# The norms' reciprocal root: Newton's rounds on GpSimd, both columns in one instruction

## The chip, the cores and the metric

The kernel runs on one core of a Trainium2 chip. Its engines are TensorE (PE in the profile; its weight loads are PEld), VectorE (DVE), ScalarE (ACT), GpSimd (POOL) and SyncE (SP, which only issues transfers here). They share SBUF; matmul results land in PSUM, which GpSimd doesn't use here. Each engine takes its instructions in the order in which they were queued, and waits on semaphores for the others. The metric is the device time of one execution in microseconds (us), the median of several runs.

## The reference, cut to what matters

Two transformer blocks run one after the other on 256 tokens of width 1024, the first with a second stream of 256 context tokens. Each has two layers. All of them normalise their input with

```python
def rms_norm(x, g):
    xf = x.astype(jnp.float32)
    y = xf * lax.rsqrt(jnp.mean(xf * xf, axis=-1, keepdims=True) + NORM_EPS)
    return (y * g.astype(jnp.float32)).astype(x.dtype)
```

For each token, then, one mean of squares and one reciprocal square root. The rest (attention of several kinds, gates, feed-forward layers) is matmuls with weights of 1024 rows and more, in float32.

## The kernel before

The residual streams lie in SBUF with the channels on the partitions: x is eight tiles of 128 channels x 256 tokens, xc is the same for the context. A weight is loaded as a raw tile and split into two parts of reduced precision, whi (a cast on ScalarE, line 200) and wlo (raw minus whi on VectorE, line 201); activations are split in the same way into hi and lo. product (lines 204 to 209) adds three matmuls for each block of 128 channels: whi with hi, whi with lo, wlo with hi. TensorE spends nearly all its time on these.

A norm goes like this. add_square sums the squares of the stream's tiles into one or two tiles sq. token_sums (line 263) brings them over the partitions with matmuls against a column of ones, so that sm holds two columns of 128 tokens each. stats_rstd (lines 266 to 274) turns them into var, -0.5 times mean plus epsilon, and calls rsqrt_columns: a start value from the bits of var by a shift and a subtraction on integers (tiles rc_s and rc_y, lines 249 and 250), and three rounds of Newton. A round is two instructions for each column, one that makes a = y * h * y (line 253) and one that makes y = (a + 1.5) * y (line 255); h is var. Then spread (line 279) transposes each column, broadcast to 128 x 128, on TensorE, so that sm holds the root of every token on all partitions, and norm (lines 311 to 317) multiplies: nt on VectorE reads sm, ScalarE makes hi, VectorE lo.

stats_rstd runs eight times, called P1 to P8 in what follows. P1 (383 us) and P2 (398 us) are the second norm of the first block's first layer, for x and for xc. P3 (764 us) and P4 (778 us) are the first norm of its second layer. P5 (993 us) is its second norm, in inner_raw, where the feed-forward matmuls start on the raw x and the root is multiplied in afterwards (fg, line 965). P6 (1216 us) and P8 (1520 us) are norms of a 128-channel key tile in the second block's two layers (ckv, line 1116). P7 (1494 us) is the norm of the second block's second layer, which is multiplied in later too. Three more calls of rsqrt_columns, one at the program's start, one between the blocks and one for the output, don't go through stats_rstd.

The order of each engine's queue isn't written out by hand. A framework schedules the program with its own estimates of how long instructions take, and code in tc.high_priority (the body of stats_rstd, wsplit) is drawn ahead of other work. So the queues can be ordered otherwise when an instruction changes its engine. The framework also sets the waits: an instruction on GpSimd that reads what the GpSimd instruction before it wrote waits for that one's semaphore.

The functions that the diff touches, and their callers:

Of the kernel before, what the change touches and what calls it, by code (L numbers as in the profile page):

```python
# [14 lines left out]
ALU = mybir.AluOpType  # L15
# [55 lines left out]
def two_blocks(ctx: ExitStack, tc: tile.TileContext, A, out: bass.AP, tap=None):  # L71
    nc = tc.nc
    V, SC, PE, GP = nc.vector, nc.scalar, nc.tensor, nc.gpsimd
# [166 lines left out]
            V.scalar_tensor_tensor(out=y, in0=a, scalar=1.5, in1=y, op0=ALU.add, op1=ALU.mult)  # L240
        return y

    def rsqrt_columns(h, name):

        n = h.shape[-1]
        sh = small.tile([P, n], I32, name=f"rc_s_{name}", tag=f"rc_s_{name}")
        y, a = (small.tile([P, n], F32, name=f"rc_{t}_{name}", tag=f"rc_{t}_{name}") for t in "ya")

        V.tensor_scalar(out=sh, in0=h.bitcast(I32), scalar1=1, scalar2=None, op0=ALU.logical_shift_right)
        V.tensor_scalar(out=y.bitcast(I32), in0=sh, scalar1=-1.0, scalar2=1597463007.0 + 1069547520.0, op0=ALU.mult, op1=ALU.add)  # L250
        for _ in range(3):
            for i in range(n):
                V.scalar_tensor_tensor(out=a[:, i:i + 1], in0=y[:, i:i + 1], scalar=h[:, i:i + 1], in1=y[:, i:i + 1], op0=ALU.mult, op1=ALU.mult)
            for i in range(n):
                V.scalar_tensor_tensor(out=y[:, i:i + 1], in0=a[:, i:i + 1], scalar=1.5, in1=y[:, i:i + 1], op0=ALU.add, op1=ALU.mult)
        return y

    def token_sums(tiles, b, c0=0, nt=2):

        for m, sq in enumerate(tiles):  # L260
            for i in range(nt):

                PE.matmul(b[:, c0 + i:c0 + i + 1], lhsT=sq[:, i * P:(i + 1) * P], rhs=ones[:, 0:1],
                          start=m == 0 and i == 0 and c0 == 0, stop=m == len(tiles) - 1, skip_group_check=True)

    def stats_rstd(tiles, denom, name="n"):

        b = sm_bank()
        token_sums(tiles, b)

        with tc.high_priority(offset=400):
            v = small.tile([P, 2], F32, name="var", tag="var")
            V.tensor_scalar(out=v, in0=b[:, :2], scalar1=-0.5 / denom, scalar2=-0.5 * EPS, op0=ALU.mult, op1=ALU.add)
            return rsqrt_columns(v, name)

    def spread(o, r, nt):

# [23 lines left out]
    def norm(s, hs, gain, shift=None, rstd=None, R=None):  # L301

        if R is None:
            r = stats_rstd(sumsq[s, 0], D) if rstd is None else rstd
            R = sm_bank()
            spread(R, r, 2)
        sl = slice(s * S, (s + 1) * S)
        for k in range(KD):
            t = narrow_tile("nt")
            hi, lo = hs[0][k][:, sl], hs[1][k][:, sl]  # L310
            V.scalar_tensor_tensor(out=t, in0=streams[s][k], scalar=gain(k), in1=R[:, :S], op0=ALU.mult, op1=ALU.mult)
            if shift is None:
                SC.copy(out=hi, in_=t)
                V.tensor_sub(out=lo, in0=t, in1=hi.bitcast(F32))
            else:
                SC.activation(out=hi, in_=t, func=AF.Identity, bias=shift(k), scale=1.0)  # L316
                V.scalar_tensor_tensor(out=lo, in0=t, scalar=shift(k), in1=hi.bitcast(F32), op0=ALU.add, op1=ALU.subtract)
# [130 lines left out]
    v = small.tile([P, 4], F32, name="var2", tag="var2")  # L448
# [5 lines left out]
    V.tensor_add(out=v, in0=v, in1=mv[:, :, 1])  # L454
    V.tensor_scalar(out=v, in0=v, scalar1=-0.5, scalar2=-0.5 * EPS, op0=ALU.mult, op1=ALU.add)
    r4 = rsqrt_columns(v, "f")
    Rp = pt_bank()
    spread(Rp, r4, 4)
# [208 lines left out]
    for l in range(DEPTH):  # L667
# [262 lines left out]
        for part, (f0, fn) in enumerate(((0, 8), (8, 8), (16, 6))):  # L930
            us = ([], [])
            for j2 in range(fn // 2):
# [18 lines left out]
                def inner_raw(u):  # L951

                    hi, lo = tiles[u]
                    bg, bu = acc()[:, :S + 2], sc_bank()[:, :S + 2]
                    product(bg, ws[2 * u], raws, KD, slice(0, S + 2))
                    product(bu, ws[2 * u + 1], raws, KD, slice(0, S + 2))
                    if not Rs:
                        R = sm_bank()
                        spread(R, stats_rstd(sumsq[0, 0], D), 2)
                        Rs.append(wide("Rs")[:, :S])  # L960
                        SC.copy(out=Rs[0], in_=R[:, :S])
                    cc = small.tile([P, 2], F32, name="shifts", tag="shifts")
                    g, t = wide("fg")[:, :S], wide("ft")[:, :S]
                    V.tensor_copy(out=cc[:, 0:1], in_=bg[:, S:S + 1])
                    V.tensor_mul(out=g, in0=bg[:, :S], in1=Rs[0])
                    SC.activation(out=g, in_=g, func=AF.Identity, bias=cc[:, 0:1], scale=1.0)
                    SC.activation(out=t, in_=g, func=AF.Tanh, scale=0.5)
                    V.scalar_tensor_tensor(out=t, in0=t, scalar=1.0, in1=g, op0=ALU.add, op1=ALU.mult)
                    V.tensor_copy(out=cc[:, 1:2], in_=bu[:, S:S + 1])
                    V.tensor_mul(out=g, in0=bu[:, :S], in1=Rs[0])  # L970
                    V.scalar_tensor_tensor(out=t, in0=g, scalar=cc[:, 1:2], in1=t, op0=ALU.add, op1=ALU.mult)
                    SC.copy(out=hi[:, :S], in_=t)
                    V.tensor_sub(out=lo[:, :S], in0=t, in1=hi[:, :S].bitcast(F32))
# [36 lines left out]
    v = small.tile([P, 4], F32, name="var2", tag="var2")  # L1010
    V.tensor_scalar(out=v, in0=b[:, :4], scalar1=-0.5 / D, scalar2=None, op0=ALU.mult)
    V.tensor_scalar(out=v[:, 0:2], in0=v[:, 0:2], scalar1=-0.5 * EPS, scalar2=None, op0=ALU.add)
    V.scalar_tensor_tensor(out=v[:, 2:4], in0=v[:, 0:2], scalar=EPS, in1=v[:, 2:4], op0=ALU.mult, op1=ALU.add)
    r4 = rsqrt_columns(v, "f")
    b1s.close()


    with tc.tile_pool(name="b2", bufs=1) as b2:
# [47 lines left out]
        for l in range(DEPTH):  # L1066
# [6 lines left out]
            if l == 0:  # L1073
                norm(0, hs, lambda k: gfw[:, k:k + 1], rstd=r4[:, 2:4])
                R = y_bank()
                spread(R, r4, 2)
            else:
                r4 = stats_rstd(sumsq[0, 0], D)
                norm(0, hs, lambda k: g_norm_2[1][:, k:k + 1], rstd=r4)
# [471 lines left out]
```

## Time and profile before

| What | Value |
|---|---|
| median of 3 runs | 1812.01 us (1809.88 to 1813.35) |
| profiled execution | 1806.31 us, its span 1804.5 us |
| TensorE busy | 1757.9 us (97%) |
| VectorE busy | 1304.5 us (72%), 2791 instructions |
| ScalarE busy | 913.8 us (51%) |
| GpSimd busy | 36.8 us (2%), 67 instructions |
| mean granted TensorE clock | 0.993 of full speed |

The profiled execution is one run; its span lasts from the first instruction to the last. Busy shares are of the span. TensorE's matmuls overlap, and their ends are modelled, so the start-to-start distance says more than the duration of one. The GpSimd rows are its constants, its transfers, sixteen small copies and eight subtractions.

### The profile page before, as it was taken

To read this page: it belongs to the slowest core of one execution; us is meant where nothing else is said; L and a number is where in the kernel's file an instruction comes from. 1 tells how busy PE (TensorE), PEld (TensorE's weight loads), DVE (VectorE), ACT (ScalarE), POOL (GpSimd) and SP (SyncE) were. 2 spreads that over 40 slices of the span, in tenths; PEclk is the share of its full clock that TensorE was granted. 3 is DMA by queue.
4 is the path that set the end of the run, shared out by engine and by line. 5 is a ranking of instruction groups with operands and counts; after the bars stand their busy time and mean duration, and the time that the engine had idled before them with its cause. 6 is when DMAs were issued, how large, how long until landed. Compare 5 with 4: busy or idle time off the path is not lost.

```text
span 1804.5 us, 29803 instructions
## 1 busy us (share of the span) xinstructions
PE 1757.9 (97%) x11553; PEld 1512.7 (84%) x11553; DVE 1304.5 (72%) x2791; ACT 913.8 (51%) x1728; POOL 36.8 (2%) x67
## 2 busy tenths in 40 slices
PE   7999999999999999999899999999999999999998
PEld 3666677798888888877699999988999998999996
DVE  6887877984657555698657756689876777986775
ACT  2578873333212212357755544465665456475444
POOL 1000000000000000000000000002000000100000
PEclk9999999999999999999999999999999999999999
DMA  9342426532444444434237455556535555544453
GB/s 315 114 111 65 129 86 167 175 129 94 140 146 163 153 155 155 145 107 142 87 105 204 157 190 187 164 163 186 164 122 164 164 187 164 177 142 135 151 187 117
DMA packets 248061, 270.89 MB, mean 150 GB/s; under 512 B 17886, under 2 KB 208720, under 8 KB 247920
## 3 DMA queue, kind: packets, MB, share of 16 engines
q1 hardware_dynamic: 246736, 267.28, 47.1%
q0 software_dynamic: 1184, 1.71, 0.6%
q8 instruction: 91, 1.49, 0.3%
q14 instruction: 50, 0.41, 0.1%
HBM read 267.90 MB, written 1.06 MB: 149 GB/s over the span
## 4 chain that ended last, share of the span: by engine, by line
PE 78%; DVE 10%; DMA 6%; ACT 4%; issue 2%; SPq 0%; ACTq 0%; DVEq 0%
PE acc L207 16%; PE acc L208 16%; PE acc L209 16%; PE sc L209 4%; PE sc L207 4%; PE sc L208 4%; DMA raw<-in_w_ffn_up_dram 3%; DVE wlo L201 3%; PE sc L590 3%; PE y L652 2%; PE pt L646 2%; ACT whi L200 2%; PE acc L1041 1%; PE acc L1040 1%; PE acc L1039 1%
## 5 line engine op out<-in xcount | busy, mean ns | idle before, releaser
L200 ACT CAST whi<-raw 128x1024 fp32r<-128x1024 f32 (+2 forms) x416 | 396.6, 959 | 601.0 <-PE acc L208 313.8
L201 DVE TENSOR_TENSOR wlo<-raw,whi 128x1024 fp32r<-128x1024 f32 (+2 forms) x416 | 458.7, 1109 | 212.3 <-ACT whi L200 207.0
L207 PE MATMUL acc<-hi,whi 128*128 128x256 f32 (+1 forms) x1920 | 590.4, 308 | 4.4 <-ACT hi L316 3.2
L208 PE MATMUL acc<-lo,whi 128*128 128x256 f32 (+1 forms) x1920 | 587.9, 307 | 0.1
L209 PE MATMUL acc<-hi,wlo 128*128 128x256 f32 (+1 forms) x1920 | 586.9, 306 | 0.9 <-DVE wlo L201 0.9
L207 PEld LDWEIGHTS acc<-hi,whi 128*128 128x128 f32 x1920 | 362.0, 189 | 25.5 <-issue 4.6
L208 PEld LDWEIGHTS acc<-lo,whi 128*128 128x128 f32 x1920 | 362.0, 189 | 19.9 <-issue 3.0
L209 PEld LDWEIGHTS acc<-hi,wlo 128*128 128x128 f32 x1920 | 362.2, 189 | 19.0 <-issue 2.4
L209 PE MATMUL sc<-hi,wlo 128*128 128x256 f32 (+1 forms) x392 | 130.5, 333 | 0.2 <-DVE wlo L201 0.2
L207 PE MATMUL sc<-hi,whi 128*128 128x256 f32 (+1 forms) x392 | 130.7, 333 | 0.0
L208 PE MATMUL sc<-lo,whi 128*128 128x256 f32 (+1 forms) x392 | 130.5, 333 | 0.0
L418 DVE SCALAR_TENSOR_TENSOR araw<-araw,silu 128x512 f32<-128x512 f32 x140 | 104.4, 746 | 26.8 <-DMA araw<-in_w_ada_dram 26.5
L209 PEld LDWEIGHTS sc<-hi,wlo 128*128 128x128 f32 x392 | 73.8, 188 | 8.7 <-DVE wlo L201 0.6
L207 PEld LDWEIGHTS sc<-hi,whi 128*128 128x128 f32 x392 | 73.8, 188 | 8.1
L208 PEld LDWEIGHTS sc<-lo,whi 128*128 128x128 f32 x392 | 73.8, 188 | 8.0
L594 DVE TENSOR_REDUCE nm<-sc 128x1 f32<-128x512 f32 (+1 forms) x96 | 56.2, 595 | 29.0 <-PE sc L590 24.6
L207 PE MATMUL acc<-uh,whi 128*128 128x256 f32 (+1 forms) x216 | 71.8, 332 | 1.8 <-ACT uh L948 1.8
L208 PE MATMUL acc<-ul,whi 128*128 128x256 f32 (+1 forms) x216 | 71.3, 330 | 0.8 <-DVE ul L949 0.6
L209 PE MATMUL acc<-uh,wlo 128*128 128x256 f32 (+1 forms) x216 | 71.0, 329 | 0.0
L418 DVE SCALAR_TENSOR_TENSOR asum<-araw,silu,asum 128x512 f32<-128x512 f32 x84 | 62.6, 745 | 7.6 <-DMA araw<-in_w_ada_dram 7.5
L646 PE MATMUL pt<-consts,pr 128*128 128x128 f32 x320 | 56.8, 286 | 5.7 <-ACT pr L629 2.2
L590 PE MATMUL sc<-ks,qst 128*128 128x512 f32 (+1 forms) x192 | 57.2, 391 | 1.8 <-ACT pr L619 1.6
(523 smaller groups left out, 3012.9 us busy)
## 6 DMA issues: line engine op xcount, KB each, us to landing
raw<-in_w_in_dram SPq DMA_DIRECT2D x89, 1024.0 KB, 5.3
araw<-in_w_ada_dram SPq DMA_DIRECT2D x160, 256.0 KB, 2.7
raw<-in_w_ffn_gate_dram SPq DMA_DIRECT2D x22, 1024.0 KB, 5.3
raw<-in_w_ffn_up_dram SPq DMA_DIRECT2D x22, 1024.0 KB, 6.5
raw<-in_w_out_dram SPq DMA_DIRECT2D x16, 1024.0 KB, 5.5
raw<-in_w_ffn_down_dram SPq DMA_DIRECT2D x16, 1024.0 KB, 4.8
raw<-in_w_branch_dram SPq DMA_DIRECT2D x12, 1024.0 KB, 5.0
raw<-in_w_in_dram SPq DMA_DIRECT2D x16, 512.0 KB, 5.2
```

The source lines that it names most:

```text
L200: SC.copy(out=h, in_=src)
L201: V.tensor_sub(out=l_, in0=src, in1=h.bitcast(F32))
L207: PE.matmul(o, lhsT=w[0][:, k, :], rhs=xs[0][k][:, sl], start=first, stop=False)
L208: PE.matmul(o, lhsT=w[0][:, k, :], rhs=xs[1][k][:, sl], start=False, stop=False)
L209: PE.matmul(o, lhsT=w[1][:, k, :], rhs=xs[0][k][:, sl], start=False, stop=last)
L418: V.scalar_tensor_tensor(out=sums_[s_], in0=r, scalar=c, in1=sums_[s_], op0=ALU.mult, op1=ALU.add)
L590: PE.matmul(sp, lhsT=qst[:, b, qt * P:(qt + 1) * P], rhs=ks[b][z][:, ko:ko + nk], start=z == 0, stop=z == 1 and not band)
L594: V.tensor_reduce(out=nm[:, b:b + 1], in_=sp, axis=AX.X, op=ALU.max, negate=True)
L646: PE.transpose(bk[:, c:c + P], prs[b][:, (t0 + t) * P:(t0 + t + 1) * P], ident)
L652: PE.matmul(y[64 * b:64 * b + 64, :], lhsT=v[:, vt0 + t, 64 * b:64 * b + 64], rhs=p[:, t, b].rearrange("p q c -> p (q c)"), start=t == 0, ...
L1039: PE.matmul(bs[t], lhsT=hs[0][k][:, sl], rhs=ws[0][:, kk, :], start=k == 0, stop=False)
L1040: PE.matmul(bs[t], lhsT=hs[1][k][:, sl], rhs=ws[0][:, kk, :], start=False, stop=False)
```

## The change

rsqrt_columns takes an engine as a third argument. stats_rstd passes GpSimd, the three other callers pass none and keep the old rounds. With an engine, the shift and the integer start value stay on VectorE, and each of the three rounds is four instructions on the engine, over both columns at a time: y * y, times h, plus 1.5, times y. So 12 instructions of one column on VectorE become 12 of two columns on GpSimd, at each of the eight places. All lines behind move down by six.

```diff
-    def rsqrt_columns(h, name):
+    def rsqrt_columns(h, name, eng=None):
...
-        for _ in range(3):
+        for _ in range(3 if eng else 0):
+
+            eng.tensor_mul(out=a, in0=y, in1=y)
+            eng.tensor_mul(out=a, in0=a, in1=h)
+            eng.tensor_scalar(out=a, in0=a, scalar1=1.5, scalar2=None, op0=ALU.add)
+            eng.tensor_mul(out=y, in0=a, in1=y)
+        for _ in range(0 if eng else 3):
             for i in range(n):
                 V.scalar_tensor_tensor(out=a[:, i:i + 1], in0=y[:, i:i + 1], scalar=h[:, i:i + 1], in1=y[:, i:i + 1], op0=ALU.mult, op1=ALU.mult)
...
-            return rsqrt_columns(v, name)
+            return rsqrt_columns(v, name, GP)
```

VectorE's queue at P1 before; xc is the context stream's residual, nt the first product of the norm, which waits for the spread:

```order
L273 TENSOR_SCALAR var<-sm 128x2
L249 TENSOR_SCALAR rc_s_n<-var 128x2
L250 TENSOR_SCALAR rc_y_n<-rc_s_n 128x2
L253 SCALAR_TENSOR_TENSOR rc_a_n<-rc_y_n,var 128x1 x2
L255 SCALAR_TENSOR_TENSOR rc_y_n<-rc_a_n,rc_y_n 128x1 x2
L253 SCALAR_TENSOR_TENSOR rc_a_n<-rc_y_n,var 128x1 x2
L255 SCALAR_TENSOR_TENSOR rc_y_n<-rc_a_n,rc_y_n 128x1 x2
L253 SCALAR_TENSOR_TENSOR rc_a_n<-rc_y_n,var 128x1 x2
L255 SCALAR_TENSOR_TENSOR rc_y_n<-rc_a_n,rc_y_n 128x1 x2
L871 SCALAR_TENSOR_TENSOR xc_107<-sc,hgate_205,xc_107 128x256
L311 SCALAR_TENSOR_TENSOR nt<-x_81,gain_0_203,sm 128x256
```

VectorE's queue at the same place now:

```order
L279 TENSOR_SCALAR var<-sm 128x2
L249 TENSOR_SCALAR rc_s_n<-var 128x2
L250 TENSOR_SCALAR rc_y_n<-rc_s_n 128x2
L877 SCALAR_TENSOR_TENSOR xc_107<-sc,hgate_205,xc_107 128x256
L317 SCALAR_TENSOR_TENSOR nt<-x_81,gain_0_203,sm 128x256
```

The twelve round instructions are gone from here, and nt stands two rows behind the start value. They stand in GpSimd's queue, right behind the last transfer of the program's start; this is that transfer, a library call and the first of three rounds of P1:

```order
L137 DMA st<-in_ml_conv_w_dram 64x128
L253 ISA
L253 TENSOR_TENSOR rc_a_n<-rc_y_n 128x2
L254 TENSOR_TENSOR rc_a_n<-rc_a_n,var 128x2
L255 TENSOR_SCALAR rc_a_n<-rc_a_n 128x2
L256 TENSOR_TENSOR rc_y_n<-rc_a_n,rc_y_n 128x2
```

Each instruction but the first of a chain waits for the one before it on GpSimd; the library call stood ahead of the first subtraction of line 1167 before.

VectorE's queue at P4 before, from var to the second round; wlo is a weight's lower part, araw a running sum of another weight (line 418):

```order
L273 TENSOR_SCALAR var<-sm 128x2
L201 TENSOR_TENSOR wlo<-raw,whi 128x1024
L249 TENSOR_SCALAR rc_s_n<-var 128x2
L418 SCALAR_TENSOR_TENSOR araw<-araw,silu 128x512
L250 TENSOR_SCALAR rc_y_n<-rc_s_n 128x2
L201 TENSOR_TENSOR wlo<-raw,whi 128x1024
L253 SCALAR_TENSOR_TENSOR rc_a_n<-rc_y_n,var 128x1 x2
L255 SCALAR_TENSOR_TENSOR rc_y_n<-rc_a_n,rc_y_n 128x1
L201 TENSOR_TENSOR wlo<-raw,whi 128x1024
L255 SCALAR_TENSOR_TENSOR rc_y_n<-rc_a_n,rc_y_n 128x1
L253 SCALAR_TENSOR_TENSOR rc_a_n<-rc_y_n,var 128x1 x2
L255 SCALAR_TENSOR_TENSOR rc_y_n<-rc_a_n,rc_y_n 128x1 x2
```

VectorE's queue at P4 now:

```order
L279 TENSOR_SCALAR var<-sm 128x2
L201 TENSOR_TENSOR wlo<-raw,whi 128x1024
L249 TENSOR_SCALAR rc_s_n<-var 128x2
L201 TENSOR_TENSOR wlo<-raw,whi 128x1024
L250 TENSOR_SCALAR rc_y_n<-rc_s_n 128x2
L201 TENSOR_TENSOR wlo<-raw,whi 128x1024 x2
L317 SCALAR_TENSOR_TENSOR nt<-xc_102,gain_1_202,sm 128x256
```

Two wlo stand ahead of the start value now, where it was one wlo and araw, and two more between it and nt.

TensorE's queue at P7 before, with buffer numbers, around the spread (line 279); the last sums stand 18 matmuls ahead of it:

```order
L1039 MATMUL acc_15989<-whi_16008,rh_15716 128x512
L1040 MATMUL acc_15989<-whi_16008,rl_15717 128x512
L1041 MATMUL acc_15989<-wlo_16009,rh_15716 128x512
L1039 MATMUL acc_15989<-whi_16008,rh_15753 128x512
L1040 MATMUL acc_15989<-whi_16008,rl_15754 128x512
L1041 MATMUL acc_15989<-wlo_16009,rh_15753 128x512
L279 MATMUL sm_15953<-consts_75,rc_y_n_15937 128x128 x2
L1039 MATMUL acc_15988<-whi_16026,rh_15792 128x512
```

TensorE's queue at P7 now:

```order
L1047 MATMUL acc_15988<-wlo_16009,rh_15753 128x512
L1045 MATMUL acc_15989<-whi_16008,rh_15716 128x512
L285 MATMUL sm_15953<-consts_75,rc_y_n_15937 128x128 x2
L1046 MATMUL acc_15989<-whi_16008,rl_15717 128x512
L1047 MATMUL acc_15989<-wlo_16009,rh_15716 128x512
L1045 MATMUL acc_15989<-whi_16008,rh_15753 128x512
```

The spread moved ahead of five matmuls. At P2 to P6 it moved ahead of 6, 17, 19, 9 and 10; at P1 and P8 it stands where it stood.

## Rows read from the trace of the kernel before

**Rows 1.** The page, part 1: engine, busy us, share of span, instructions.

```profile
PE 1757.9 (97%) x11553; PEld 1512.7 (84%) x11553; DVE 1304.5 (72%) x2791; ACT 913.8 (51%) x1728; POOL 36.8 (2%) x67
```

**Rows 2.** By tile rc_y_n: engine, operation, count, ns shortest/median/longest, first and last start.

```profile
L253 DVE SCALAR_TENSOR_TENSOR rc_a_n<-rc_y_n,var x48: 209/213/220, 383.2 to 1521.9; 128x1 f32<-128x1 f32 x48
L255 DVE SCALAR_TENSOR_TENSOR rc_y_n<-rc_a_n,rc_y_n x48: 136/153/163, 383.5 to 1522.1; 128x1 f32<-128x1 f32 x48
```

**Rows 3.** Timeline at P1: start us, us, engine, instruction, count, [idle before, releaser].

```profile
382.45 0.36 PE L207 MATMUL sc<-hi,whi 128*128 128x256 f32 x1
...
383.02 0.17 DVE L250 TENSOR_SCALAR rc_y_n<-rc_s_n 128x2 int32<-128x2 int32 x1
...
384.40 0.28 DVE L255 SCALAR_TENSOR_TENSOR rc_y_n<-rc_a_n,rc_y_n 128x1 f32<-128x1 f32 x2
...
384.67 0.20 PEld L279 LDWEIGHTS sm<-consts,rc_y_n 128*128 128x128 f32 x2 [0.29 <-PE acc L207]
```

**Rows 4.** By windows: us, then PE, PEld, DVE, ACT, POOL busy, PEclk, DMA, GB/s.

```profile
380.00:390.00 10.00, 9.88 (x85) 9.71 (x84) 7.20 (x25) 3.33 (x5) 0.00 (x0) 1.00 0.04 14
```

**Rows 5.** GpSimd by line and shape: count, busy us, mean ns, idle before.

```profile
L1030 POOL MEMSET wk<- 128x512 f32 x1 | 0.5, 526 | 0.0
...
L1529 POOL MEMSET const-float32-1.0<- 128x1 f32 x1 | 0.1, 98 | 0.0
```

**Rows 6.** By source line, 1221 and 1167: GpSimd's copies and subtractions, columns as rows 2.

```profile
L1221 POOL COPY khat<-krw x16: 391/472/684, 1225.1 to 1534.3; 16x256 f32<-16x256 f32 x16
...
L1167 POOL TENSOR_TENSOR dm<-dm,bfs x8: 673/920/1177, 1239.5 to 1683.7; 128x256 f32<-128x256 f32 x8
```

**Rows 7.** Timeline of GpSimd: two copies, the second waiting for the first.

```profile
1225.13 0.47 POOL L1221 COPY khat<-krw 16x256 f32<-16x256 f32 x1 [34.77 <-ACT khat L1218]
...
1225.66 0.48 POOL L1221 COPY khat<-krw 16x256 f32<-16x256 f32 x1
```

**Rows 8.** Timeline of VectorE and GpSimd near 1380 us.

```profile
1379.76 1.23 DVE L201 TENSOR_TENSOR wlo<-raw,whi 128x1024 fp32r<-128x1024 f32 x1 [0.67 <-ACT whi L200]
...
1380.37 1.16 POOL L1167 TENSOR_TENSOR dm<-dm,bfs 128x256 f32<-128x256 f32 x1 [6.18 <-DMA dm<-mxd]
```

**Rows 9.** Timeline at P3: start value, first nt, TensorE's wait for hi.

```profile
764.18 0.17 DVE L250 TENSOR_SCALAR rc_y_n<-rc_s_n 128x2 int32<-128x2 int32 x1
...
769.19 1.65 DVE L311 SCALAR_TENSOR_TENSOR nt<-x,gain,sm 128x256 f32<-128x256 f32 x4
...
771.06 0.51 PE L207 MATMUL acc<-hi,whi 128*128 128x256 f32 x2 [1.43 <-ACT hi L316]
```

**Rows 10.** Timeline at P4: var, last round, first nt, TensorE's wait for hi.

```profile
778.00 0.16 DVE L273 TENSOR_SCALAR var<-sm 128x2 f32<-128x2 f32 x1 [1.07 <-PE sm L263]
...
783.40 0.28 DVE L255 SCALAR_TENSOR_TENSOR rc_y_n<-rc_a_n,rc_y_n 128x1 f32<-128x1 f32 x2
784.14 1.66 DVE L311 SCALAR_TENSOR_TENSOR nt<-xc,gain,sm 128x256 f32<-128x256 f32 x4 [0.47 <-PE sm L279]
...
786.15 0.54 PE L207 MATMUL acc<-hi,whi 128*128 128x512 f32 x1 [1.81 <-ACT hi L316]
```

**Rows 11.** The chain that ended last, in order of time, behind P5: start, us, what.

```profile
1002.77 5.67 DMA raw<-in_w_ffn_up_dram
```

**Rows 12.** Timeline at P7: the matmul behind the sums, start value, spread.

```profile
1493.69 0.48 PE L1039 MATMUL acc<-whi,rh 128*128 128x512 f32 x1
...
1494.54 0.17 DVE L250 TENSOR_SCALAR rc_y_n<-rc_s_n 128x2 int32<-128x2 int32 x1
...
1498.03 0.40 PE L279 MATMUL sm<-consts,rc_y_n 128*128 128x128 f32 x2
```

**Rows 13.** By windows, columns as rows 4: behind P4's spread, and ahead of P5.

```profile
785.00:789.00 4.00, 2.85 (x7) 1.94 (x8) 4.00 (x10) 3.27 (x7) 0.00 (x0) 0.68 0.82 210
789.00:793.00 4.00, 4.00 (x17) 3.19 (x16) 4.00 (x14) 1.78 (x4) 0.00 (x0) 0.89 0.02 4
986.00:990.00 4.00, 1.95 (x13) 1.43 (x12) 3.40 (x6) 1.46 (x3) 0.00 (x0) 1.00 0.34 99
```

## The prediction

> **What bounds the kernel now.** The page's first part says TensorE: busy 97% of the span [rows 1]. So a microsecond is lost or won only where TensorE waits, and each place was read by two questions: when does TensorE reach an instruction, and when is its operand ready? The change touches eight places, one for each call of stats_rstd: 48 and 48 round instructions on rc_y_n, from 383.2 to 1522.1 us, are 8 calls of 6 and 6 [rows 2]. They are called P1 to P8 here, in order of time. At each, TensorE sums squares, VectorE makes rc_y_n in two integer steps and three rounds, and two transposes on TensorE (the spread) wait for it. Whatever is queued behind the spread on TensorE waits too, though it needs nothing of it.
>
> At P1 the first matmul behind the sums starts at 382.45, the start value of the root is done at 383.19, the last round at 384.68, and the spread's weight load starts at 384.67 after an idle 0.29 us [rows 3]. So the 12 instructions take 1.49 us, and a cover of 16 matmuls, 1.93 us, hides all but 0.29. Around P1 85 matmuls start in 10 us: 0.118 us each [rows 4].
>
> **What goes.** 96 VectorE instructions, 12 at each place, some 1.5 us each time [rows 3]: about 12 us of VectorE work. None of it is TensorE time, and VectorE takes its queue in strict order: its next instruction that needs the spread (nt, ckv or fg) stands a few rows behind, so most of what is freed turns into waiting there. I count it at nothing except at P3 and P4.
>
> **What comes: a chain on GpSimd.** 12 instructions of 128x2, each waiting for the one before. The trace has none of that shape, so it is bounded. Below: a MEMSET of one column, 98 ns, which reads nothing [rows 5]; above: the shortest COPY of 256 columns, 391 ns, taken whole [rows 6]. Between: MEMSET costs (526-98)/511 = 0.84 ns a column [rows 5]; taking that from COPY leaves 391-214 = 177 ns, and twice that (two inputs) from the shortest two-input instruction leaves 673-429 = 244 ns [rows 6]. Three of four instructions in a round have two inputs, so I take 0.22 us. A copy that waits for the copy before it starts 0.06 us behind its end [rows 7]. That gives 0.28 us a step and 3.36 us a chain, with ends of 12 x (0.098+0.06) = 1.9 and 12 x (0.391+0.06) = 5.4. The library call in front of the first chain stands in GpSimd's queue behind the DMA issues of the program's start, long ahead of its first use; counted at nothing.
>
> [...]
>
> **Collisions.** A GpSimd subtraction starts at 1380.37 while VectorE's wlo (two inputs in SBUF) runs from 1379.76 to 1380.99: it takes 1.16 us and ends 0.54 behind wlo's end [rows 8], against 0.673 at best [rows 6]. So a wlo that lies beside the chain costs it up to a wlo (1.23), and nothing if it falls clear; I take 0.8 each. By the order, no such instruction stands between start value and spread at P1 and P2, one wlo at P5 to P8, one wlo and one araw at P3 (0.8 + 0.6), two wlo at P4 (1.6).
> [...]
>
> **What moves.** The spread now stands nearer to the sums on TensorE: 16, 17, 16, 28, 16, 24, 13 and 19 matmuls behind them, where it was 16, 23, 33, 47, 25, 34, 18 and 19. The cover shrinks while the chain grows. The moved matmuls are not lost; they come behind the spread.
>
> **The sum.** From the first matmul behind the sums to the start value it is 0.74 us at P1 [rows 3], and the same three short VectorE instructions elsewhere; 0.05 more to wake GpSimd (estimate, from the 0.06 above). The cover is 0.04 + 0.118 for each matmul, so that 16 give 1.93.
> - P1: 0.79 + 3.36 - 1.93 = 2.2, less the 0.29 of before: +1.9.
> - P2: 17 matmuls, 2.05: +2.1.
> - P3 and P4 differ: TensorE already waits there for hi of the normed x, 1.43 and 1.81 us [rows 9, 10]. So the path is start value, chain, spread, nt, hi, and the moved matmuls fill the old waits. P3: 764.35 + 0.05 + 3.36 + 1.4 = 769.16 is the new chain's end; at P4 nt starts 0.46 behind the last round's end [rows 10], with the first use of a fresh spread I allow 0.65, so nt starts at 769.8 against 769.19 [rows 9]: +0.6. P4: VectorE now has two wlo ahead of the start value, so it is done near 780.6 (778.00, two wlo of 1.13 from start to start, and the short ones); the chain ends at 780.6 + 3.36 + 1.6 = 785.6, against 783.68 [rows 10]: +1.9.
> - P5: 0.79 + 3.36 + 0.8 - 1.93 = 3.0. Here the chain of waits soon runs through a transfer of 5.67 us [rows 11], so TensorE's later waits take some back; I count half: +1.5.
> - P6: 24 matmuls, 2.87: +2.1.
> - P7: matmuls of 512 columns; 18 of them lie between 1493.69 and 1498.03, 0.241 each, so 13 are 3.13. The start value is done at 1494.71, 1.02 behind [rows 12]: 1.02 + 0.05 + 3.36 + 0.8 - 3.13 = +2.1.
> - P8: 19 matmuls, 2.28: +2.7.
>
> Together +14.9 us. **The clock** adds to it. [...] In 986 to 990 TensorE is busy for only 1.95 of 4 us and the clock stays at 1.00 [rows 13]. So new waits of 2 to 3 us may or may not do it; I count two more such falls, +3.4; ends none and six (+10). Sum +18.3.
>
> The profiled run took 1806.31 us, its span 1804.5 with 1.8 around it; with the sum 1824.6. The timed median is 1812.01, 5.7 above the profiled run; the trace does not say why, and I put the difference on the median: **1830**.
>
> **Rivals.**
> - *Short chain, no change.* At 0.16 to 0.18 a step and few collisions the chain is about 2 us: P1, P2, P5 and P8 lose 0.4 to 0.9 each, P3 and P4 gain 1.1 to 1.4, the rest nothing: with P4's clock fall gone or not, between -2 and +3, 1810 to 1815. For it: the 98 ns row. Against: that row reads nothing.
> - *Faster.* One mechanism: hi comes earlier at P3 and P4, because the rounds no longer stand between wlo and araw on VectorE [rows 9, 10]. It can give at most the two waits, 1.43 + 1.81, and P4's clock fall, 1.7: about -5, 1807. It decides from a chain under 2.05 us without collisions (0.17 a step), where the gains at P3 and P4 cancel the losses of the others. Against it: rows 8.
> - *Slow GpSimd.* If the fixed cost is COPY's 391 ns whole, a step is 0.45 and the chain 5.4 us: 2.0 more at seven and a half places, +15, and two more clock falls, +3.4: 1849. For it: a copy has one input, a round mostly two. [...]
> - That the change doesn't do what it says: by the order 96 arithmetic instructions stand on GpSimd and none on VectorE for these calls; no chance given.
>
> **How the numbers follow.** Forecast 0.68 (1817 to 1841), slow GpSimd 0.17, no change 0.10, faster 0.05. The forecast's own ends: a step of 0.20 takes 0.96 off each of seven and a half places (-7), few collisions another 5; a step of 0.33 adds 4.5, full collisions 2, two more clock falls 3.4. The range of 8 in 10 takes in half of the slow rival and the upper edge of no change: 1814 to 1846. A measurement of this kernel tells about 0.2% (3.6 us) from no change; beyond it: faster 0.04, within 0.11, slower 0.85.
>
> **What would show it.** On GpSimd: eight chains of 12, a step of 0.25 to 0.32 us, longer where wlo runs. On TensorE: waits of 1.5 to 3 us ahead of the spread at P1, P2 and P5 to P8, released by GpSimd; at P3 and P4 the wait for hi turned into one ahead of the spread. VectorE some 12 us less busy, and idle ahead of nt. I am wrong if a step is under 0.18 us, if TensorE's waits at the spread are below 1 us, or if waits later in the program shrink by what these grow.

## The result, and the profile after

| | before | after |
|---|---|---|
| median of 4 runs | 1811.99 us (1809.88 to 1813.35) | 1833.79 us (1827.99 to 1835.25) |
| profiled execution, its span | 1806.31, 1804.5 us | 1827.99, 1826.2 us |
| ratio, 95% interval | | 1.0112, 1.0097 to 1.0127 |

The change costs 20.3 us by the ratio (17.6 to 23.0) and 21.8 by the medians; 18.3 were forecast over the profiled run, 18.0 over the median. The first part of the page (busy time, share of the span, instructions):

```profile
PE 1759.6 (96%) x11553; PEld 1515.8 (83%) x11553; DVE 1295.1 (71%) x2695; ACT 912.8 (50%) x1728; POOL 63.4 (3%) x163
```

TensorE has the same work to 2 us in a span that is 21.7 us longer, so it waits 20.0 us more. VectorE lost 96 instructions and 9.4 us, GpSimd gained 96 and 26.6. What TensorE waits for (total, times, longest, us), the first row:

```profile
PE sm L285 <- POOL rc_y_n L256: 21.1, 8, 3.7
```

Eight times, once at each place, the spread waits for the last step on GpSimd: 2.05, 1.91, 3.48, 3.67, 3.09, 2.17, 2.06 and 2.71 us at P1 to P8. At P1 and P8 the spread stands where it stood, so that all of the wait comes from the longer chain; at P2 to P7 the 5 to 19 matmuls that it was moved ahead of, 66 in all, took cover away as well. GpSimd at P1 (start, duration, then the idle time before and what ended it):

```profile
385.32 0.19 POOL L253 TENSOR_TENSOR rc_a_n<-rc_y_n 128x2 f32<-128x2 f32 x1 [337.82 <-DVE rc_y_n L250]
385.59 0.20 POOL L254 TENSOR_TENSOR rc_a_n<-rc_a_n,var 128x2 f32<-128x2 f32 x1
385.88 0.21 POOL L255 TENSOR_SCALAR rc_a_n<-rc_a_n 128x2 f32<-128x2 f32 x1
386.17 0.19 POOL L256 TENSOR_TENSOR rc_y_n<-rc_a_n,rc_y_n 128x2 f32<-128x2 f32 x1
386.45 0.19 POOL L253 TENSOR_TENSOR rc_a_n<-rc_y_n 128x2 f32<-128x2 f32 x1
...
388.42 0.20 POOL L256 TENSOR_TENSOR rc_y_n<-rc_a_n,rc_y_n 128x2 f32<-128x2 f32 x1
```

A round is 385.32 to 386.45, 1.13 us, four steps of 0.28; the chain ends at 388.62, after 3.30 us. The twelve on VectorE before took 1.49 [rows 3]. TensorE at the same place:

```profile
386.35 0.28 PE L207 MATMUL acc<-hi,whi 128*128 128x256 f32 x1
388.67 0.43 PE L285 MATMUL sm<-consts,rc_y_n 128*128 128x128 f32 x2 [2.05 <-POOL rc_y_n L256]
388.86 0.36 PE L208 MATMUL acc<-lo,whi 128*128 128x256 f32 x1
```

It stands for 2.05 us in front of the spread, with a product behind it that needs no norm, and goes on 0.05 us after the chain's end. At P4, VectorE first and then GpSimd:

```profile
787.33 1.22 DVE L201 TENSOR_TENSOR wlo<-raw,whi 128x1024 fp32r<-128x1024 f32 x1
788.47 0.16 DVE L250 TENSOR_SCALAR rc_y_n<-rc_s_n 128x2 int32<-128x2 int32 x1
788.54 2.35 DVE L201 TENSOR_TENSOR wlo<-raw,whi 128x1024 fp32r<-128x1024 f32 x2
```

```profile
788.71 1.10 POOL L253 TENSOR_TENSOR rc_a_n<-rc_y_n 128x2 f32<-128x2 f32 x1 [13.22 <-DVE rc_y_n L250]
789.89 1.06 POOL L254 TENSOR_TENSOR rc_a_n<-rc_a_n,var 128x2 f32<-128x2 f32 x1
791.03 0.21 POOL L255 TENSOR_SCALAR rc_a_n<-rc_a_n 128x2 f32<-128x2 f32 x1
```

Each of the two wlo holds one step: 1.10 and 1.06 us in place of 0.19 and 0.20, 0.9 more each. Such long steps stand at P3 to P8, none at P1 and P2: eight of them, which make the chains 6.9 us longer in all, about a third of the 21.1 us of waits. At P5 (TensorE, then the window around it: its width, the busy time and count of PE, PEld, DVE, ACT and POOL, the granted clock, the DMA share, GB/s):

```profile
1006.04 0.69 PE L285 MATMUL sm<-consts,rc_y_n 128*128 128x128 f32 x2 [3.09 <-POOL rc_y_n L256]
...
1007.60 0.42 PE L207 MATMUL acc<-rh,whi 128*128 128x258 f32 x1
...
1009.43 0.29 PE L207 MATMUL sc<-rh,whi 128*128 128x258 f32 x1
```

```profile
1002.00:1010.00 8.00, 4.91 (x29) 4.70 (x29) 3.17 (x7) 3.23 (x6) 3.08 (x12) 0.79 0.10 32
```

Behind the wait the matmuls take 0.42 us until the clock is back, and 0.29 from then on. The granted clock is 0.50 in 1006:1009 and 1.00 in 1009.3:1010; a mean of 0.79 over 8 us is 1.7 us lost. In before the window 993:1002 around P5 had 1.00.

### The profile page after: what moved, and what is told of

The parts are those of the page before. It is cut to its first block, busy times and chain, and to the rows that moved or that the text cites. A ratio compares the mean times of both kernels' runs of the same rounds, so it can differ in the third digit from the quotient of the medians.

```text
span 1826.2 us, 29813 instructions
## 1 busy us (share of the span) xinstructions
PE 1759.6 (96%) x11553; PEld 1515.8 (83%) x11553; DVE 1295.1 (71%) x2695; ACT 912.8 (50%) x1728; POOL 63.4 (3%) x163
## 3 DMA queue, kind: packets, MB, share of 16 engines
q8 instruction: 91, 1.49, 0.3%
HBM read 267.90 MB, written 1.06 MB: 147 GB/s over the span
## 4 chain that ended last, share of the span: by engine, by line
PE 77%; DVE 9%; DMA 6%; ACT 4%; issue 2%; POOL 1%; SPq 0%; ACTq 0%; DVEq 0%; POOLq 0%
PE acc L208 15%; PE acc L207 15%; PE acc L209 15%; PE sc L209 4%; PE sc L207 4%; PE sc L208 4%; DVE wlo L201 3%; PE sc L596 2%; PE y L658 2%; DMA raw<-in_w_ffn_up_dram 2%; PE pt L652 2%; DMA araw<-in_w_ada_dram 2%; ACT whi L200 1%; PE acc L1047 1%; PE acc L1046 1%
## 5 line engine op out<-in xcount | busy, mean ns | idle before, releaser
L207 PEld LDWEIGHTS acc<-hi,whi 128*128 128x128 f32 x1920 | 362.9, 189 | 21.7 <-issue 3.8
```

The costliest lines, as they stand in the source:

```text
L207: PE.matmul(o, lhsT=w[0][:, k, :], rhs=xs[0][k][:, sl], start=first, stop=False)
```

## The experiments

The theory (T): a chain of 3.3 us, lengthened by wlo beside it, is exposed where TensorE reaches the spread too soon; a clock fall follows some of the waits. Against it stand the order of the queues (R1), the form of the rounds on whatever engine (R2), and the collisions as the main part (R3). Costs below are the ratio's excess, with its interval, over the runs of before on the same chip.

**The same form on VectorE.**

```diff
-            return rsqrt_columns(v, name, GP)
+            return rsqrt_columns(v, name, V)
```

> The changed kernel with one word put back: the same four instructions a round over both columns, but on VectorE. Theory T (the exposed length of the GpSimd chain, 3.3 us from the start value to the spread, is the loss): twelve dependent instructions of the 0.15 to 0.21 us that before's rounds took make 2 to 2.5 us, and the scheduler puts 21 to 53 matmuls (2.5 to 6 us) ahead of each spread instead of 13 to 28, so that six or more of the eight waits of the spread go and the time is before's within 4 us, 1808 to 1816. Rival R2 (it is the form, twelve dependent steps of both columns where before had six pairs, on whichever engine): waits of 2 us or more stay at most places, 1825 or above. Rival R1 (the rounds leave VectorE's queue, and the new order of the queues costs): the order is near before's again, so about 1812; T and R1 agree here.

Measured: 1818.12 us against 1812.51, ratio 1.0026 (1.0009 to 1.0043): +4.7 us (1.6 to 7.8). Most of the loss is gone, but not all, and the median lies 2 us above T's range. So R2 is right in part. VectorE at P1, and then at P3:

```profile
384.97 0.16 DVE L253 TENSOR_TENSOR rc_a_n<-rc_y_n 128x2 f32<-128x2 f32 x1
385.17 0.16 DVE L254 TENSOR_TENSOR rc_a_n<-rc_a_n,var 128x2 f32<-128x2 f32 x1
385.36 0.17 DVE L255 TENSOR_SCALAR rc_a_n<-rc_a_n 128x2 f32<-128x2 f32 x1
385.57 0.16 DVE L256 TENSOR_TENSOR rc_y_n<-rc_a_n,rc_y_n 128x2 f32<-128x2 f32 x1
...
768.68 0.16 DVE L256 TENSOR_TENSOR rc_y_n<-rc_a_n,rc_y_n 128x2 f32<-128x2 f32 x1
768.83 1.22 DVE L201 TENSOR_TENSOR wlo<-raw,whi 128x1024 fp32r<-128x1024 f32 x1
769.97 0.15 DVE L253 TENSOR_TENSOR rc_a_n<-rc_y_n 128x2 f32<-128x2 f32 x1
```

A step is 0.20 us from start to start, 0.28 on GpSimd. The run changes the cover with the step: the spread stands 21 to 53 matmuls behind the sums here, so it doesn't show alone what the shorter step is worth. At P3 three wlo, two araw and three updates of xc stand between the start value and the last step, so these take from 767.09 to 774.66, and TensorE waits 2.73 us for the spread and 1.17 for hi, against 1.43 before [rows 9]; at P4 1.59 and 1.58 against 1.81 [rows 10]. That is 3.8 us more at the two places, of the size of the whole cost: the twelve steps cost on VectorE where its queue puts other work between them. At the other six the waits are 0.3 or less.

**Two rounds, and six.** The first leaves out the third round of Newton, the second adds three.

```diff
-        for _ in range(3 if eng else 0):
+        for _ in range(2 if eng else 0):
```

> The changed kernel with two rounds on GpSimd instead of three; the third round of Newton is left out. T: the chain is 8 steps of 0.275 us, 2.2 us, 1.1 shorter at each place; the spread stands 3 to 12 matmuls nearer to the sums at most places (0.35 us or more less cover), so a place wins 0.4 to 0.9 us: 3 to 7 us in all, 1826 to 1831. R1 (the order of queues): no more than 1 us, 1833. R3 (collisions): one of the 12 steps meets a long instruction at six places; with 8 steps nearly as many, so 0 to 2 us, 1832 to 1834.

> The changed kernel with six rounds on GpSimd instead of three; the time of the chain is doubled. T: 12 more steps of 0.275 us are 3.3 us at each place, less 5 to 11 matmuls more ahead of the spread (0.6 to 1.3 us): 2.0 to 2.7 us a place, 16 to 22 us in all, 1850 to 1856; a clock fall more would add 1.7 us. R1 (the order, not the length): 1834 to 1838. R3 (collisions): the doubled chain meets another long instruction at most of six places, 1 us each, 1838 to 1842.

Measured: two rounds 1828.03, 1.0075 (1.0046 to 1.0105), +13.6 us (8.3 to 19.0); six 1862.05, 1.0261 (1.0225 to 1.0297), +47.3. The waits of the spread, two rounds and then six:

```profile
PE sm L285 <- POOL rc_y_n L256: 12.0, 8, 2.3
PE acc L209 <- DVE wlo L201: 6.7, 3, 5.7
```

```profile
PE sm L285 <- POOL rc_y_n L256: 40.7, 8, 6.1
```

12.0, 21.1 and 40.7 us for chains of 8, 12 and 24 steps: each step more adds 1.6 to 2.3 us over the eight places, as T has it. The time follows, with two additions. With two rounds one new wait of 5.7 us for a wlo came at P4, where VectorE's queue now has that wlo behind many nt and lo; so the order of the queues does matter at one place, and the gain is about 6 us (5.8 by the medians) and not 9; its interval just overlaps that of three rounds (17.6 to 23.0). With six the time grew by 27 us over the change, 5 beyond T's range, 19.6 of them the waits; the clock took more (a mean of 0.980 in the profile, 0.991 with three rounds). Its windows behind the wait of P1:

```profile
385.00:393.00 8.00, 2.86 (x26) 2.66 (x24) 1.87 (x3) 1.05 (x1) 5.79 (x24) 0.84 0.00 0
393.00:400.00 7.00, 7.00 (x43) 7.00 (x44) 4.97 (x10) 2.33 (x4) 0.00 (x0) 0.69 0.06 9
```

0.16 x 8 + 0.31 x 7 = 3.5 us, where the clock stood at 1.00 in before and with three rounds. The 5.14 us of wait there were followed by about twice the loss that P5's 3.09 brought.

**The spread at the end of the independent matmuls.**

```diff
-            spread(R, r, 2)
+            with tc.high_priority(offset=-140):
+                spread(R, r, 2)
```

The spreads in inner_raw and for ckv are put under the same line.

> The changed kernel, rounds still on GpSimd, but the transposes of the root (spread) are scheduled later: 63, 47, 45, 31, 72, 33, 90 and 36 matmuls stand between the sums and the spread at P1 to P8, where the changed kernel has 16, 17, 16, 28, 16, 24, 13 and 19. T: a place needs about 0.8 us for the start value, 3.3 for the chain and up to 1.1 for a wlo beside it, 4.1 to 5.2 us or 35 to 44 matmuls of 0.118 us; so the waits at P1, P2, P3, P5 and P7 go, P4, P6 and P8 keep at most 1.5 us each, and what waits behind the norm at P3 and P4 (hi) may wait as much as before (1.4 to 1.8 us). 12 to 18 of the 22 us come back: 1815 to 1822. R1 (order of the queues or the instructions moved, not the wait of the spread): 5 us or less comes back, 1828 or above. R3 (the collisions of a GpSimd step with a two-input VectorE instruction beside it are the main part): the collisions stay, and 1828 or above too, unless they are hidden likewise; the waits of the spread tell it.

Measured: 1837.81, 1.0135 (1.0101 to 1.0169), +24.5 us: nothing came back, a miss for T as it stood. TensorE at P2:

```profile
406.50 0.28 PE L209 MATMUL sc<-hi,wlo 128*128 128x256 f32 x1
406.61 0.43 PE L285 MATMUL sm<-consts,rc_y_n 128*128 128x128 f32 x2
408.22 0.39 PE L207 MATMUL acc<-hi,whi 128*128 128x256 f32 x1 [1.17 <-ACT hi L323]
```

The spread's wait is gone, and 1.17 us for hi stand behind it: nothing is left to cover nt and hi. The matmuls that don't need the norm are one stock, and what is put ahead of the spread is missing behind it. In all, the spread still waits 9.9 us in four places. Elsewhere the waits for wlo grew from 2.1 us in four places to 5.5 in ten, and one for rl from 0.7 to 3.1; which reordering made each was not separated.

**The spread in the middle.**

```diff
+    later = [70, 105, 75, 150, 60, 0, 90, 70, 90]
+
+    def late_spread(o, r):
+
+        with tc.high_priority(offset=-later.pop(0) if later else 0):
+            spread(o, r, 2)
...
-            spread(R, r, 2)
+            late_spread(R, r)
```

The two other spreads call late_spread too.

> The changed kernel, rounds on GpSimd, with the transposes of the root put in the middle of the matmuls that need no norm: 34, 34, 36, 41, 48, 33, 38 and 33 matmuls stand ahead of them at P1 to P8 (changed kernel: 16, 17, 16, 28, 16, 24, 13, 19), each place with its own distance. The run with the transposes at the end of these matmuls (63, 47, 45, 31, ...) showed the wait of the spread gone at P1 and P2 and one of 1.2 to 1.5 us for hi in its place, since nt and hi after the spread had nothing left beside them. T (the chain is exposed as far as the matmuls that don't need the norm run out, on either side of the spread): from var, the root comes at 4.0 us at P1 and P2 and 5.0 at the others, 34 to 42 matmuls, and the norm's own product 1.9 us after it, so the waits of the spread at P1, P2, P5 and P7 go, P3, P4, P6 and P8 keep about 1 us each, in all 10 to 15 of the 22 us come back: 1818 to 1824. R1 (the queues' order or the moved instructions): 1830 or above.

Measured: 1824.64 against 1813.71, 1.0070 (1.0045 to 1.0094): +12.7 us (8.2 to 17.0), so some 8 to 9 us came back.

```profile
PE sm L285 <- POOL rc_y_n L256: 11.5, 7, 2.4
```

The spread's waits fell from 21.1 to 11.5 us, 9.6, and the time by about as much: with the same chain and the same collisions it is the wait that is paid for. R1's 1830 is not reached. The median is 0.6 us over T's range, and P1 (0.94) and P2 (1.99, its start value came 1.2 us later) kept waits that T had gone.

**The collisions without the wait.** Before's rounds stay on VectorE, and 13 dependent steps on GpSimd are read by nobody.

```diff
-            return rsqrt_columns(v, name, GP)
+            y = rsqrt_columns(v, name)
+            w = small.tile([P, 2], F32, name="shadow", tag=f"rc_s_{name}")
+            GP.tensor_mul(out=w, in0=v, in1=v)
+            for _ in range(3):
+                GP.tensor_mul(out=w, in0=w, in1=v)
+                GP.tensor_scalar(out=w, in0=w, scalar1=0.0, scalar2=None, op0=ALU.mult)
+                GP.tensor_mul(out=w, in0=w, in1=v)
+                GP.tensor_mul(out=w, in0=w, in1=w)
+            return y
```

> The kernel before, its rounds on VectorE and its queues of TensorE as they were (16, 23, 33, 47, 25, 34, 18, 19 matmuls ahead of the spread), and beside them a chain of 13 dependent instructions of 128x2 on GpSimd at each of the eight places that starts from var and that nothing reads. It has the collisions of the change, and not its wait. T: nothing waits for it; VectorE's instructions beside it are delayed by 0.2 us or less each, and the time is before's, 1811 to 1814. R3 (the cost is what GpSimd and VectorE do to each other): six collisions of about 1 us at the places, 1817 or above.

Measured: 1814.15 against 1813.71, 1.0005 (0.9992 to 1.0019). GpSimd's tile and VectorE's wlo (count, shortest, median and longest in ns):

```profile
L285 POOL TENSOR_SCALAR shadow<-shadow x24: 212/213/1247, 385.7 to 1532.7; 128x2 f32<-128x2 f32 x24
L286 POOL TENSOR_TENSOR shadow<-shadow,var x24: 194/198/1257, 386.0 to 1533.0; 128x2 f32<-128x2 f32 x24
```

```profile
L201 DVE TENSOR_TENSOR wlo<-raw,whi x416: 680/1218/1415, 66.8 to 1775.1; 128x1024 fp32r<-128x1024 f32 x110, 128x512 fp32r<-128x512 f32 x25, 128x768 fp32r<-128x768 f32 x4
```

Steps of over 1 us are there as in the change, and in all the collisions lengthen GpSimd's steps by 12.8 us here, by 6.9 in the change. wlo's median is 1218 ns, 1218 with the change and 1217 before; the eleven 128x1024 wlo with a step of GpSimd's beside them took 1211 to 1226 ns, the others 1220 in the median. GpSimd pays the collision, VectorE nothing that shows. R3 falls in the form that GpSimd's mere presence costs; the collisions cost only as steps of a chain that is waited for.

**One group of places at a time.** P1 and P2; P5; P3 and P4; P6 to P8.

```diff
+    places = []
+
     def stats_rstd(tiles, denom, name="n"):
...
-            return rsqrt_columns(v, name, GP)
+            places.append(name)
+            return rsqrt_columns(v, name, GP if len(places) < 3 else None)
```

The others have `len(places) == 5`, `in (3, 4)` and `> 5`.

> The rounds on GpSimd at P1 and P2 alone, where no collision was; the six others on VectorE as before, with before's 33, 47, 25, 34, 18 and 19 matmuls ahead of their spreads. T: the two places cost what the changed kernel's trace shows for them, 2.0 and 2.4 us: 1816.3, between 1815 and 1818. R3 (collisions are the main part): here there are none, and the time is before's, within 1 us of 1812. R1 (the order further on): also near 1812, since the order further on is before's.

> The rounds on GpSimd at P5 alone, the seven others as before; 16 matmuls instead of 25 ahead of the spread there. The prediction charged P5 with 1.5 us, half of its arithmetic, and the changed kernel lost 4.8 between P5 and P6, two clock falls among it. T with the whole wait: 3.0 us, and one clock fall of 1.7 us behind it if the pause itself sets it off: 1815 to 1817. If half of the wait is given back by work that is late anyway, as the prediction had it: 1813.5. If the loss in that stretch came from what the earlier places had moved, and not from P5: within 1 us of 1812.

> The rounds on GpSimd at P3 and P4 alone, the six others as before; 16 and 28 matmuls instead of 33 and 47 ahead of the two spreads. The prediction's terms were 0.6 and 1.9 us. In the trace of the changed kernel the two places together cost 1.2 us of lag, although TensorE waits 3.5 and 3.7 us for the two spreads: the waits for hi of 1.4 and 1.8 us there were before are gone, and something else gives time back. T with the waits alone: 3.5 + 3.7 - 1.4 - 1.8 = 4.0 us, 1817 to 1819. By the lag: 1814 to 1816. If the two waits only take the place of what was late anyway: 1812 to 1814.

> The rounds on GpSimd at P6, P7 and P8 alone, the five others as before; 24, 13 and 19 matmuls ahead of the three spreads. T: the waits of the spread that the changed kernel shows there are 2.2, 2.1 and 2.7 us, 7.0 in all, and one clock fall: 7 to 9 us over before, 1820 to 1824. If the places add up (4.6 us for P1 and P2, 3.1 for P5, and this and the run with P3 and P4 alone), the four runs together give the 22 us of the whole change; so about 10 us here if P3 and P4 give 4. If the losses at the places feed each other, the sum of the four falls short of 22 by 4 us or more.

| places | forecast, clock apart | waits of the spread | median, us | ratio (95%) | cost, us |
|---|---|---|---|---|---|
| P1, P2 | 4.0 | 4.0 | 1818.29 | 1.0029 (1.0015 to 1.0044) | 5.3 (2.7 to 8.0) |
| P3, P4 | 2.5 | 7.1, less hi's 3.2 of before | 1818.71 | 1.0035 (1.0023 to 1.0048) | 6.3 (4.2 to 8.7) |
| P5 | 1.5 | 3.1 | 1816.85 | 1.0018 (1.0001 to 1.0034) | 3.3 (0.2 to 6.2) |
| P6 to P8 | 6.9 | 7.0 | 1821.50 | 1.0042 (1.0028 to 1.0056) | 7.6 (5.1 to 10.2) |
| sum | 14.9 | 18.0 | | | 22.5 |

The four sum to 22.5 us, the change to 20.3 (17.6 to 23.0): the places add up, within an uncertainty of the sum of some 5 us, so that a small effect of one place on another isn't excluded. By the medians P1 and P2 came 0.3 us over T's range and the three others inside theirs; P3 and P4 cost more than the lag of the changed kernel's trace had given, and P5's interval leaves its half wait open. P1 and P2, without any collision, cost their share, which again speaks against R3; and the order further on is before's there, against R1. The waits of the spread in the runs with P1 and P2, P5, P3 and P4, and P6 to P8:

```profile
PE sm L288 <- POOL rc_y_n L256: 4.0, 2, 2.1
```

```profile
PE sm L288 <- POOL rc_y_n L256: 3.1, 1, 3.1
```

```profile
PE sm L288 <- POOL rc_y_n L256: 7.1, 2, 3.7
```

```profile
PE sm L288 <- POOL rc_y_n L256: 7.0, 3, 2.7
```

The windows around P3 and P4 in the run with these two alone, and then around P4 in before:

```profile
765.00:775.00 10.00, 6.52 (x43) 6.32 (x42) 4.47 (x10) 1.73 (x3) 3.81 (x12) 0.75 0.46 148
783.00:797.00 14.00, 9.87 (x63) 9.46 (x63) 9.39 (x19) 4.15 (x8) 4.16 (x12) 0.77 0.52 150
```

```profile
778.00:793.00 15.00, 13.12 (x73) 11.02 (x73) 14.53 (x43) 8.60 (x16) 0.00 (x0) 0.89 0.54 159
```

0.25 x 10 + 0.23 x 14 = 5.7 us lost to the clock, against 0.11 x 15 = 1.7 in before (1.00 in its window 764:773, 0.89 in 778:793). In the changed kernel's own run the clock fell at P4 and not at P3, so a fall may or may not follow a wait of 3.5 us. The same holds for the 2.05 us at P1: 1.00 in 385:390 of the changed kernel, 0.79 in the run of P1 and P2 alone. P3 in the changed kernel, and P1 in that run:

```profile
770.00:776.00 6.00, 2.52 (x21) 2.32 (x21) 2.77 (x6) 1.05 (x1) 3.69 (x12) 1.00 0.34 104
```

```profile
385.00:393.00 8.00, 5.95 (x38) 5.74 (x38) 3.68 (x7) 1.56 (x2) 2.01 (x10) 0.79 0.00 0
```

No kernel here beats the kernel before.

## Why the prediction was right, point by point

- **TensorE's waits are what counts: right.** TensorE's idle time grew by 20.0 us in the profiled execution; the spread's waits are 21.1 of what stands there now, and 3.2 for hi at P3 and P4 have gone. That is 18 us where the sum had 14.9, and nearly all of the difference lies at P3 and P5 (below).
- **A step of 0.28 us, a chain of 3.36: right.** 0.27 to 0.30 and 3.30. The value between the MEMSET of one column and the shortest COPY [rows 5, 6] came out at 0.19 to 0.21 against 0.22 taken, and the gap of the two copies [rows 7] at 0.08. The short-chain rival had 0.18 a step at most, the slow one 0.45. The same two-input instruction on two columns takes 0.16 us on VectorE (the form on VectorE) and 0.19 to 0.20 on GpSimd, a ratio of 1.2.
- **Collisions, 0.8 each: right, slightly small.** A wlo adds 0.9 to 1.0 us to one step, an araw 0.4 at P3. At P4 a step of 0.19 takes 1.10 beside a wlo that began 0.17 us before it. No step here shows VectorE held: the wlo beside the long steps take 1.22 to 1.23 us, 1.22 in the median of all.
- **P1, P2, P6, P7, P8: right.** 1.9, 2.1, 2.1, 2.1, 2.7 forecast; 2.05, 1.91, 2.17, 2.06, 2.71 waited.
- **P3 and P4, +0.6 and +1.9: right at P4, mis-sized at P3.** From var to nt it is 5.40 and 6.14 us before [rows 9, 10; var at P3 starts at 763.79] and 5.85 and 8.28 after, 0.45 and 2.1 more, and the waits for hi went as foreseen. TensorE's wait grew by 1.86 us at P4 (3.67 for 1.81), but by 2.05 at P3 (3.48 for 1.43). There the bill isn't nt's delay: hi was ready before TensorE had done the matmuls that were moved behind the spread, as the rows below show, so what it lost is its wait ahead of the spread. Alone the two places cost 6.3 us (4.2 to 8.7), not 2.5. Beyond the waits (3.9 more) it is the clock, which these two terms don't hold: in the profile of this run 4.0 us more were lost there to it, and over its timed runs the mean granted clock is 0.990, against 0.992 in the runs of before on that chip. Two hi at P3 in the changed kernel, then the first matmul that uses one:

```profile
778.15 0.91 ACT L322 ACTIVATE hi<-nt,mod 128x256 fp32r<-128x256 f32 x2
```

```profile
779.24 0.28 PE L207 MATMUL acc<-hi,whi 128*128 128x256 f32 x1
```

- **P5, +1.5: mis-sized.** The arithmetic gave 3.0, the trace a wait of 3.09, and no run speaks for halving it because the chain of waits soon runs through a transfer [rows 11]. Alone, P5 cost 3.3 us (0.2 to 6.2), by which 1.5 isn't excluded; the clock fell at the wait's end in both runs (0.79 in 1002:1010 of the changed kernel, 0.66 in 1000:1005 of the run with P5 alone).
- **Two more clock falls, +3.4: not decided.** The 1.7 us of one fall are what the two windows behind P4's spread lose by their granted clock [rows 13], 1.3 and 0.4; P5 lost 1.7 too. How many a change of this size adds no run shows. The stretches at half clock (granted 0.50), without the program's end, add up to 27 us in the profile after and 20 in that of before, at P5 and P6 as new ones. But the profile with the shadow chain has 27 as well, at before's time, so such a difference between single executions is no evidence; runs of before differ by several us among themselves (1806.86 to 1822.18 over 29). Over the timed runs the mean granted clock is 0.986 to 0.991 with the change and 0.988 to 0.996 in those 29, so something more is lost to it, but how much at which place isn't shown. A fall that lies directly behind a spread's wait, as at P5, is charged to it here.
- **VectorE 12 us less busy, counted at nothing: right.** It is 9.4 less busy, and no time came of it; in the view of the tile rc_y_n, nt is among those that wait:

```profile
who waited for it (us, times):
  POOL rc_a_n L253: 921.4, 8
  PEld sm L285: 23.0, 8
  PE sm L285: 21.1, 8
  DVE nt L317: 12.5, 5
```

VectorE stands 12.5 us for the spread ahead of nt, at five places, more than it was relieved of.

## What to carry to other kernels

Moving a small chain of dependent instructions to an idle engine took 9.4 us of busy time off VectorE here and cost 20.3 us, where the chain's latency wasn't hidden: count the work between the instruction that starts the chain and the one that needs its end, and price the chain by its start-to-start distance. The work that could cover it was one stock for the chain and for everything behind it up to the next use: moving the consumer to its end only moved the wait (+24.5 us), moving it to the middle gave 8 to 9 us of the loss back. When a place pauses TensorE, add what the clock may take behind it: here it fell behind some waits of 1.8 to 5.1 us and not behind others.

## What had not been expected of the hardware

- The prediction's row of a collision had two inputs. A one-input TENSOR_SCALAR on GpSimd is held by a wlo on VectorE likewise: 212 ns at best, 1247 at worst, in the run with the shadow chain, and 1.08 to 1.23 us beside a wlo at P6 to P8 in the changed kernel; the median of VectorE's wlo stays at 1218 ns.
- The time of a tiny instruction is much alike on both engines: 0.19 to 0.21 us for 128x2 on GpSimd, 0.16 to 0.17 on VectorE. What differs more is the gap between dependent ones, 0.08 against 0.03 to 0.04 us, so that a step is 0.28 against 0.20.
- The clock fall that follows a wait is not sure: after the 3.5 us at P3, and after the 2.05 at P1, it came in one run and not in another. Its size differs too: 1.7 us lost behind the 3.09 at P5, 3.5 behind the 5.14 at P1 with six rounds.
